# Attention over normalised queries and keys on one core: one reciprocal for both heads of a pair, and a new order

## The chip, the cores and the metric

The kernel runs on one core of a Trainium2 chip. The metric is the device time of the whole kernel in microseconds. The core has five engines that run side by side, each taking its own instructions strictly in order: TensorE (PE in the profile, its weight loads as PEld), VectorE (DVE), ScalarE (ACT), GpSimd (POOL) and SyncE (SP, which here only starts transfers). They wait for each other through semaphores.

## The reference

Eight batches of twelve heads, 512 positions, 64 dimensions, `tau` = 0.1:

```python
Q_norm = Q / (np.linalg.norm(Q, axis=-1, keepdims=True) + 1e-10)
K_norm = K / (np.linalg.norm(K, axis=-1, keepdims=True) + 1e-10)
scores = np.einsum('bhqd,bhkd->bhqk', Q_norm, K_norm) / tau
weights = np.exp(scores - np.max(scores, axis=-1, keepdims=True))
weights = weights / (np.sum(weights, axis=-1, keepdims=True) + 1e-10)
return np.einsum('bhqk,bhkd->bhqd', weights, V).astype(np.float32)
```

The scores are bounded by 10, so the kernel leaves out the maximum. It divides by the sum of the weights at the very end, after the product with V.

## The kernel before

**Tiling.** The 96 heads are worked off as 48 pairs of neighbouring heads, numbered 0 to 47 (`s` in the code; `h` is the head within a pair). 512 positions are four tiles of 128.

**One pair.** The steps have the names that the code gives them in `P.add`:

- `LD s.0`, `LD s.1`, `LV s` (SP): the transfers of Q, K and V into rings of buffers; a ring's size says how many pairs later a buffer is used again (`RINGS`: 17 for Q and K, 8 for V).
- `SQ` (POOL mostly), `SSQ` (PE, eight small products that sum the squares of K in groups) and `RED` (DVE): sums of squares. For Q, `RED` alone works on 512 columns.
- `NEW` steps (DVE, lines 419 to 430): the inverse root by Newton's method, for groups of two or four pairs at once, up to eight small instructions.
- `SCL s.0`, `SCL s.1` (DVE or POOL, line 451): scaling of Q and K. `TR s.0`, `TR s.1` (PE, line 457): four transposes each. `EVA s` (DVE, line 465): their copy out of PSUM.
- `SCO s.c` (PE, line 551), c = 0 to 3: scores of one key tile for both heads, two matmuls. `EXP s.c` (ACT, line 567): the exponential of those 128x1024 scores. Scores have four PSUM banks, so two chunks are held at a time. One chunk, `43.3`, is not done on ACT but as a polynomial on DVE and POOL (`SCX`, `X`, `Y`).
- `VC s` (POOL, line 575): V to bf16 with a column of ones next to the 64 of V.
- `PV s.h.i` (PE, line 587), i = 0 to 3: weights times V for one query tile, four matmuls of 65 columns. Column 65 is the sum of the weights. All four tiles of head h lie in one PSUM bank, `o_ps[h]`; the two banks are the halves of the tile `ops` (`both` in the code). The `SSQ` products use free columns of the same banks.
- `RCP s.h` (DVE, line 599): the reciprocal of the four sums of a head. `NRM s.h` (DVE, line 604): the product of the 128x256 result with them, into the buffer `ob` (a ring of 8). `ST s` (SP, line 608): the transfer of both heads to memory.

**What a bank waits for.** The first product of pair s + 1 in the bank of head h, `PV s+1.h.0`, waits for `NRM s.h` (and for a `RED`, where a sum of squares used that bank between). `NRM s.h` waits for `RCP s.h` and for the store of pair s - 8.

**The order.** Each engine's order is written out by hand in `ORDER` as numbers. A number is the place at which the step was registered by `P.add`, pair by pair. So the same number means another step once a registration is added or dropped. The prediction names the steps by what the numbers mean in each version, as `PV 36.0.2` for pair 36, head 0, query tile 2. `JOINT` and `ONE_PRODUCT` are lists of pairs that choose a form of `RCP` and `NRM`; before, `JOINT` is empty, and each head has its own `RCP`.

Of the kernel before, what the change touches and what calls it, by code (L numbers as in the profile page):

```python
# [5 lines left out]
ALU = mybir.AluOpType  # L6
# [102 lines left out]
def bass_cosine_similarity_attention_kernel(  # L109
# [8 lines left out]
    BATCH, NHEAD, SEQ, DIM = Q.shape  # L118
    assert SEQ == 512 and DIM == 64 and NHEAD % 2 == 0
    NT = SEQ // 128  # L120
# [4 lines left out]
    R_QK, R_V, R_VB, R_SQ, R_QN, R_QT, R_ET, R_O, R_X = RINGS  # L125
# [34 lines left out]
    P = Program(nc)  # L160
# [29 lines left out]

    def key(name, s, *rest):
        return (name, s) + rest if s >= 0 else None
# [48 lines left out]
    for s in range(NP):  # L241
        for h in range(2):
            bank_free[s, h] = before[h]
            before[h] = [("NRM", s, h)] + ([("RED",) + attached[s, h]] if (s, h) in attached else [])
# [282 lines left out]
    def rest(s):  # L527
# [54 lines left out]
        for h in range(2):  # L582
# [13 lines left out]
            ends = lambda h: [("PV", s, h, NT - 1), ("SSQ",) + attached[s, h] if (s, h) in attached else None, key("NRM", s - R_O, h)]  # L596
            if s not in JOINT:
                P.add(("RCP", s, h), "dve", "rcp", T0 + PERIOD + 0.9 * PV_AT[4 * h + 3] + late(s), ends(h),
                      lambda e, h=h, grid=grid: e.reciprocal(out=rd[io][:, h, :], in_=grid[:, :, DIM]))  # L599
            elif h == 0:  # L600
                P.add(("RCP", s), "dve", "rcp2", T0 + PERIOD + 0.9 * PV_AT[4 * h + 3] + late(s), ends(0) + ends(1),
                      lambda e: e.reciprocal(out=rd[io][:, :, :], in_=both[:, :, 0 : 65 * NT].rearrange("p h (t x) -> p h t x", x=65)[:, :, :, DIM]))
            P.add(("NRM", s, h), "dve", "nrm", T0 + PERIOD + 0.2 + 0.9 * PV_AT[4 * h + 3] + late(s), [("RCP", s) if s in JOINT else ("RCP", s, h), key("ST", s - R_O)],
# [3 lines left out]
        P.add(("ST", s), "sp", "ld", s + STORE_AT, [("NRM", s, i) for i in range(2)],  # L607
              lambda e: e.dma_start(out=src(out, s), in_=ob[io][:, :].rearrange("p h t d -> p h (t d)")), slot=f"out{io}")

    def last(s, T0):  # L610
        ivb, iet, io = s % R_VB, s % R_ET, s % R_O
        spare = t_ps[:, :, :, :].rearrange("p w t x -> p (w t x)").bitcast(f32)
        for k, (h, lo, hi) in enumerate(PIECES):
# [15 lines left out]
            P.add(("RCP", s, k), "dve", "rcp", T0 + PERIOD + 4 + k, [("PV", s, k, NT - 1), key("NRM", s - R_O, h)],  # L629
# [47 lines left out]
JOINT = ()  # L677
# [13 lines left out]
def late(s):  # L691
    return LATE * max(0.0, 1 - s / LATE_TO)


def slack(s, most):
# [14 lines left out]
    ),  # L710
    "pool": (
# [115 lines left out]
```

## Time and profile before

| | |
|---|---|
| median of 3 runs | 190.48 us (190.14 to 191.09) |
| the profiled execution | 190.63 us, of which the span (first to last instruction) 188.9 us |
| granted TensorE clock | 0.996 of full speed |
| memory | 37.75 MB read, 12.58 MB written, 267 GB/s over the span |
| transfers on SP's order | 193 |

A row of a group names the line, the engine, the operation, the tile written and the tiles read with their shapes, how often it ran, its busy time and mean duration in ns, and the idle time of the engine just before it, with what ended that. A row of the timeline has the start in us from the begin of the span, the length, and in brackets the idle time before. Instructions of one engine can overlap in their records, so the mean of a group can be longer than its share of the time.

### The profile page before, as it was taken

How to read it: one execution, taken by the hardware profiler on the slowest of the kernel's cores; microseconds unless marked ns; L12 is line 12 of the kernel's file. 1: busy time of each engine (PE TensorE's matmuls, PEld its weight loads, DVE VectorE, ACT ScalarE, POOL GpSimd, SP SyncE). 2: the span in 40 equal slices, each digit the busy share in tenths (PEclk: the TensorE clock that was granted, in tenths of full speed). 3: DMA queues.
4: the chain of work that ended last, by engine and by line, in shares of the span. 5: the costliest groups of instructions: out<-in, count | busy, mean ns of one | idle time of the engine just before them, and what ended most of it. 6: DMA issues, size and time to landing. Idle time of an engine off the chain costs nothing.

```text
span 188.9 us, 6666 instructions
## 1 busy us (share of the span) xinstructions
PE 175.7 (93%) x2710; PEld 111.0 (59%) x2710; DVE 169.3 (90%) x541; ACT 182.0 (96%) x214; POOL 160.9 (85%) x149
## 2 busy tenths in 40 slices
PE   8979889999999999999899989999999899899982
PEld 2545466656665666666566656656566566455652
DVE  1789999999999999999899998999989999998752
ACT  5699999999999999999999999999999999999993
POOL 3798999999999999999999999999999994594000
PEclk9999999999999999999999999999999999999998
DMA  5999999999997899999999999986973062200655
GB/s 182 346 353 351 349 350 374 367 378 271 293 313 264 263 310 318 263 351 357 377 363 326 374 358 365 362 302 193 333 267 115 2 222 88 86 0 3 207 186 168
DMA packets 52446, 50.76 MB, mean 269 GB/s; under 512 B 3136, under 2 KB 52416, under 8 KB 52416
## 3 DMA queue, kind: packets, MB, share of 16 engines
q1 hardware_dynamic: 51984, 50.02, 80.5%
q8 instruction: 21, 0.34, 0.8%
q10 hardware_dynamic: 432, 0.33, 0.5%
q14 instruction: 9, 0.07, 0.1%
HBM read 37.75 MB, written 12.58 MB: 267 GB/s over the span
## 4 chain that ended last, share of the span: by engine, by line
ACT 92%; PE 5%; DVE 2%; issue 0%
ACT et L567 89%; ACT et L543 2%; PE ops L205 2%; PE ops L587 1%; PE ops L619 0%; PE scps L551 0%; DVE ob L638 0%; PE tps L287 0%; PE ops L287 0%; ACT sq L360 0%; DVE xa L392 0%; DVE ob L604 0%; PE ops L385 0%; DVE qt L298 0%; DVE xa L269 0%
## 5 line engine op out<-in xcount | busy, mean ns | idle before, releaser
L567 ACT ACTIVATE et<-scps 128x1024 bf16<-128x1024 f32 x186 | 171.1, 1180 | 0.0
L368 POOL TENSOR_TENSOR sq<-qk 128x1024 bf16<-128x1024 f32 x44 | 82.7, 1893 | 0.4 <-DMA qk<-in_K_dram 0.3
L551 PE MATMUL scps<-qt 64*128 64x512 bf16 x374 | 73.0, 386 | 7.1 <-ACT et L567 3.6
L587 PE MATMUL ops<-vb,et 128*128 128x65 bf16 x1504 | 75.2, 195 | 0.5 <-DVE ob L604 0.3
L587 PEld LDWEIGHTS ops<-vb,et 128*128 128x128 bf16 x1504 | 57.1, 98 | 29.4 <-issue 17.7
L451 POOL TENSOR_TENSOR qn<-qk,rk 128x512 bf16<-128x512 f32 x38 | 39.2, 1043 | 6.4 <-DVE rk L426 6.2
L604 DVE TENSOR_TENSOR ob<-ops,rd 128x256 f32<-128x256 f32 x94 | 39.0, 419 | 1.2 <-DMA out_dram<-ob 0.5
L451 DVE TENSOR_TENSOR qn<-qk,nps 128x512 bf16<-128x512 f32 x56 | 36.9, 677 | 0.7 <-ACT nps L412 0.6
L465 DVE COPY qt<-tps 128x1024 bf16<-128x1024 bf16 x47 | 32.1, 683 | 0.8 <-PE tps L457 0.6
L457 PE MATMUL tps<-ident,qn 128*128 128x128 bf16 x376 | 32.3, 220 | 0.4 <-DVE qn L451 0.3
L551 PEld LDWEIGHTS scps<-qt 64*128 64x128 bf16 x374 | 18.4, 92 | 24.1 <-ACT et L567 8.0
L396 DVE TENSOR_REDUCE xs<-sq 128x8 f32<-128x512 bf16 x46 | 30.5, 671 | 0.2 <-POOL sq L368 0.2
L575 POOL TENSOR_SCALAR vb<-vf 128x512 bf16<-128x512 f32 x48 | 28.9, 620 | 0.2 <-DMA vf<-in_V_dram 0.2
L457 PEld LDWEIGHTS tps<-ident,qn 128*128 128x128 bf16 x376 | 21.5, 97 | 10.5 <-issue 5.2
L599 DVE RECIPROCAL rd<-ops 128x4 f32<-128x4 f32 x94 | 16.1, 174 | 5.0 <-PE ops L587 3.8
L385 PE MATMUL ops<-sq,ident 128*128 128x64 bf16 x384 | 19.0, 193 | 0.2 <-ACT sq L360 0.2
L385 PEld LDWEIGHTS ops<-sq,ident 128*128 128x128 bf16 x384 | 14.2, 98 | 4.1 <-issue 3.1
L392 DVE TENSOR_REDUCE xs<-ops 128x8 f32<-128x64 f32 x46 | 9.5, 207 | 0.6 <-PE ops L385 0.3
L419 DVE TENSOR_TENSOR ts<-xs,nps 128x32 f32<-128x32 f32 (+2 forms) x34 | 6.6, 194 | 0.6
L426 DVE SCALAR_TENSOR_TENSOR nps<-ts,nps 128x32 f32<-128x32 f32 (+3 forms) x34 | 6.7, 196 | 0.6
L422 DVE SCALAR_TENSOR_TENSOR ts<-ts,nps 128x32 f32<-128x32 f32 (+2 forms) x34 | 6.5, 190 | 0.4
L362 POOL TENSOR_TENSOR sq<-qk 128x512 bf16<-128x512 f32 x5 | 5.1, 1039 | 1.3 <-DMA qk<-in_K_dram 1.3
(62 smaller groups left out, 54.7 us busy)
## 6 DMA issues: line engine op xcount, KB each, us to landing
vf<-in_V_dram SPq DMA_DIRECT2D x48, 256.0 KB, 5.7
qk<-in_Q_dram SPq DMA_DIRECT2D x47, 256.0 KB, 4.8
qk<-in_K_dram SPq DMA_DIRECT2D x47, 256.0 KB, 5.6
out_dram<-ob SPq DMA_DIRECT2D x47, 256.0 KB, 4.7
qk<-in_Q_dram SPq DMA_DIRECT2D x2, 128.0 KB, 2.7
qk<-in_K_dram ACTq DMA_DIRECT2D x2, 128.0 KB, 2.9
out_dram<-ob SPq DMA_DIRECT2D x1, 128.0 KB, 1.7
out_dram<-ob ACTq DMA_DIRECT2D x1, 64.0 KB, 1.8
```

The source lines that it names most:

```text
L368: lambda e: e.tensor_tensor(out=sqf, in0=data, in1=data, op=ALU.mult))
L385: last = e.matmul(out=o_ps[bank][:, 320:384], lhsT=ident[:, :], rhs=sq[iqs][:, 8 * w : 8 * w + 8, 8 * k : 8 * k + 8], start=(k == 0), stop ...
L396: lambda e, w=w, dst=dst: e.tensor_reduce(out=dst, in_=sq[iqs][:, 8 * w : 8 * w + 8, :], axis=AX.X, op=ALU.add))
L451: lambda e, w=w, r=r: e.tensor_tensor(out=qn[iqn][:, w].rearrange("p t h d -> p h t d"), in0=qk[iq][:, w].rearrange("p h (t d) -> p h t d" ...
L457: last = e.transpose(t_ps[:, w, t, :], qn[iqn][:, w, t].rearrange("p h d -> p (h d)"), ident[:, :])
L465: lambda e: e.tensor_copy(out=qt[iqt][:, :, :, :].rearrange("p w t x -> p (w t x)"), in_=t_ps[:, :, :, :].rearrange("p w t x -> p (w t x)")))
L551: last = e.matmul(out=sc_ps[:, 2 * b + h, :], lhsT=qt[iqt][64 * h : 64 * h + 64, 1, c, :], rhs=qt[iqt][64 * h : 64 * h + 64, 0, :, :], sta ...
L567: lambda e, c=c, b=b: e.activation(out=et[iet][:, c, :, :], in_=sc_ps[:, 2 * b : 2 * b + 2, :], func=ACT.Exp, scale=math.log(2.0) / UNIT i ...
L575: lambda e: e.tensor_scalar(out=vb[:, ivb : ivb + n, :, :, 0:DIM].rearrange("p n h c d -> p (n h c) d"), in0=vf[:, iv : iv + n].rearrange( ...
L587: last = e.matmul(out=o_ps[h][:, 65 * t : 65 * t + 65], lhsT=et[iet][:, c, h, 128 * t : 128 * t + 128], rhs=vb[:, ivb, h, c, :], start=(c ...
L599: lambda e, h=h, grid=grid: e.reciprocal(out=rd[io][:, h, :], in_=grid[:, :, DIM]))
L604: lambda e, h=h, grid=grid: e.tensor_tensor(out=ob[io][:, h], in0=grid[:, :, 0:DIM], in1=rd[io][:, h, :].unsqueeze(2).to_broadcast([128, N ...
```

## The change

For pairs 12 to 45 there is one `RCP s` in place of `RCP s.0` and `RCP s.1`. It reads the sums of both heads, 128x8 values out of both banks, and waits for the last product of both. The two `NRM s.h` stay as they are, and both wait for the one `RCP s`. The form was in the code before (`if s not in JOINT`), with no pair in the list. The list `ONE_PRODUCT`, for one `NRM` over both heads as well, is new and empty, so that form isn't used. The helper `nrm` gives the name of the step that ends a pair's normalisation; with `ONE_PRODUCT` empty it gives what stood there before.

The orders of SP, POOL, DVE and PE are new from about the eighth pair on; ACT does the same steps in the same order as before. No transfer, product or POOL step is added or dropped. Some numbers of the lists change only because 34 registrations are gone.

```diff
+    def nrm(s, h):
+        return None if s < 0 else ("NRM", s, 0 if s in ONE_PRODUCT else h)
...
-            before[h] = [("NRM", s, h)] + ([("RED",) + attached[s, h]] if (s, h) in attached else [])
+            before[h] = [nrm(s, h)] + ([("RED",) + attached[s, h]] if (s, h) in attached else [])
...
-            ends = lambda h: [("PV", s, h, NT - 1), ("SSQ",) + attached[s, h] if (s, h) in attached else None, key("NRM", s - R_O, h)]
+            ends = lambda h: [("PV", s, h, NT - 1), ("SSQ",) + attached[s, h] if (s, h) in attached else None, nrm(s - R_O, h)]
             if s not in JOINT:
                 P.add(("RCP", s, h), "dve", "rcp", T0 + PERIOD + 0.9 * PV_AT[4 * h + 3] + late(s), ends(h),
                       lambda e, h=h, grid=grid: e.reciprocal(out=rd[io][:, h, :], in_=grid[:, :, DIM]))
             elif h == 0:
                 P.add(("RCP", s), "dve", "rcp2", T0 + PERIOD + 0.9 * PV_AT[4 * h + 3] + late(s), ends(0) + ends(1),
                       lambda e: e.reciprocal(out=rd[io][:, :, :], in_=both[:, :, 0 : 65 * NT].rearrange("p h (t x) -> p h t x", x=65)[:, :, :, DIM]))
...
-JOINT = ()
+JOINT = tuple(range(12, 46))
+ONE_PRODUCT = ()
```

Of the orders, the stretches that the prediction uses, in names:

| engine | before | after |
|---|---|---|
| PE, pair 36 to 37 | PV 36.0.2, PV 36.0.3, PV 35.1.2, PV 35.1.3, SCO 38.0, TR 39.0, TR 39.1, SCO 38.1, PV 37.0.0 | PV 36.1.2, PV 36.0.2, PV 36.0.3, PV 36.1.3, SCO 38.0, TR 39.0, TR 39.1, SCO 38.1, PV 37.0.0 |
| DVE, pair 36 | RCP 36.0, RCP 35.1, NEW, NRM 36.0, ..., RCP 36.1, SCL 40.0, NRM 36.1 | RCP 36, NEW, NEW, NRM 36.1, NRM 36.0 |
| SP, early | LV 5, LD 8.0, LD 8.1, LV 6, LD 9.0, LD 9.1, LV 7, LD 10.0, LD 10.1, LV 8 | LV 5, LD 11.1, LD 13.0, LD 8.0, LD 12.0, LD 8.1, LV 6, LD 9.0, LD 16.0, LD 9.1, LV 7, LD 10.0, LD 14.1, LD 17.1, LD 10.1, LD 21.1, LD 21.0, LD 15.0, LD 11.0, LD 16.1, LV 8 |
| SP, stores 9 to 14 in turn | 10, 9, 11, 13, 12, 14 | 12, 14, 9, 11, 10, 13 |
| POOL, pair 8 | SQ 10, VC 8, VC 6, VC 10, SCL 8.1 | SQ 10, VC 8, SCL 8.1 (VC 6 behind SQ 8, VC 10 later) |
| PE, end | SCO 47.1, PV 46.1.0, PV 46.0.0 to 46.0.3, SCO 47.2, PV 46.1.1 to 46.1.3, SCO 47.3, PV 47.1.0, PV 47.0.0, ... | SCO 47.1, PV 46.0.0, SCO 47.2, PV 46.0.1, PV 46.1.0, PV 46.0.2, PV 46.0.3, PV 46.1.1, SCO 47.3, PV 46.1.2, PV 46.1.3, PV 47.0.0, ... |

More of the change, by code (lines that the diff above doesn't have):

```diff
@@ L602, in rest @@
                       lambda e: e.reciprocal(out=rd[io][:, :, :], in_=both[:, :, 0 : 65 * NT].rearrange("p h (t x) -> p h t x", x=65)[:, :, :, DIM]))
+            if s in ONE_PRODUCT:
+                if h == 0:
+                    P.add(("NRM", s, 0), "dve", "nrm2", T0 + PERIOD + 0.2 + 0.9 * PV_AT[7] + late(s), [("RCP", s), key("ST", s - R_O)],
+                          lambda e: e.tensor_tensor(
+                              out=ob[io][:, :, :, :], in0=both[:, :, 0 : 65 * NT].rearrange("p h (t x) -> p h t x", x=65)[:, :, :, 0:DIM],
+                              in1=rd[io][:, :, :].unsqueeze(3).to_broadcast([128, 2, NT, DIM]), op=ALU.mult))
+                continue
             P.add(("NRM", s, h), "dve", "nrm", T0 + PERIOD + 0.2 + 0.9 * PV_AT[4 * h + 3] + late(s), [("RCP", s) if s in JOINT else ("RCP", s, h), key("ST", s - R_O)],
@@ L606, in rest @@
                       in1=rd[io][:, h, :].unsqueeze(2).to_broadcast([128, NT, DIM]), op=ALU.mult))
-        P.add(("ST", s), "sp", "ld", s + STORE_AT, [("NRM", s, i) for i in range(2)],
+        P.add(("ST", s), "sp", "ld", s + STORE_AT, [nrm(s, i) for i in range(2)],
               lambda e: e.dma_start(out=src(out, s), in_=ob[io][:, :].rearrange("p h t d -> p h (t d)")), slot=f"out{io}")
@@ L628, in last @@
             grid = bank[:, 0 : 65 * (hi - lo)].rearrange("p (t x) -> p t x", x=65)
-            P.add(("RCP", s, k), "dve", "rcp", T0 + PERIOD + 4 + k, [("PV", s, k, NT - 1), key("NRM", s - R_O, h)],
+            P.add(("RCP", s, k), "dve", "rcp", T0 + PERIOD + 4 + k, [("PV", s, k, NT - 1), nrm(s - R_O, h)],
                   lambda e, h=h, lo=lo, hi=hi, grid=grid: e.reciprocal(out=rd[io][:, h, lo:hi], in_=grid[:, :, DIM]))
```

149 rows, old and new, of the table ORDER are left out of this document.

## The prediction

> **What bounds the kernel now.** I read the page of the profile first: busy time by engine, then the chain that ended last, then the groups of instructions.
>
> ```profile
> span 188.9 us, 6666 instructions
> ...
> PE 175.7 (93%) x2710; PEld 111.0 (59%) x2710; DVE 169.3 (90%) x541; ACT 182.0 (96%) x214; POOL 160.9 (85%) x149
> ...
> DVE  1789999999999999999899998999989999998752
> ...
> ACT 92%; PE 5%; DVE 2%; issue 0%
> ...
> L567 ACT ACTIVATE et<-scps 128x1024 bf16<-128x1024 f32 x186 | 171.1, 1180 | 0.0
> ```
>
> Four engines look nearly full, but the chain runs through ACT for 92% of the span. Its exponentials (L567) fill 171.1 us with 0.0 us of idle time, so 171.1 / 186 = 0.920 us each. Their records (1180 ns) overlap, so a late one does not show as idle time: it shows as a longer step from start to start. For the best step I read two windows of ACT's timeline (start, length, group; each begins with the record already running):
>
> ```profile
> 99.94 11.18 ACT L567 ACTIVATE et<-scps 128x1024 bf16<-128x1024 f32 x12
> ```
> ```profile
> 108.97 2.15 ACT L567 ACTIVATE et<-scps 128x1024 bf16<-128x1024 f32 x2
> ```
>
> The first group has twelve starts and ends at 111.12, as the second does, so 108.97 is its eleventh: ten steps in 9.03 us, 0.903 each. All 186 at that step would take 168.0 us. **All that any rearrangement can win inside the exponentials is therefore 171.1 - 168.0 = 3.1 us.** The orders change from about 27 us on. The best case needs the share that lies there:
>
> ```profile
> 13.49 79.06 ACT et L567 x86
> ...
> 92.56 1.02 ACT et L567
> ...
> 93.60 88.11 ACT et L567 x96
> ```
>
> These are pieces of the chain in order of time. The first 15 of the 186 start before 27 us. The later 171 carry about their part of the 3.1 us or a little less; adding up their single steps gives 2.4 us over 0.903. I use 2.4 us as the ceiling of a gain there. The run took 190.63 us around its span of 188.9; the median of the three runs shown is 190.48, 0.15 below it. Sums below are made on 190.63 and given against the median.
>
> **Where the 2.4 us go.** The worst single one is at 91 us. ACT's, DVE's and TensorE's timelines there:
>
> ```profile
> 91.33 2.25 ACT L567 ACTIVATE et<-scps 128x1024 bf16<-128x1024 f32 x2
> ```
> ```profile
> 91.02 0.42 DVE L604 TENSOR_TENSOR ob<-ops,rd 128x256 f32<-128x256 f32 x1 [0.48 <-DMA out_dram<-ob]
> ```
> ```profile
> 91.51 0.68 PE L587 MATMUL ops<-vb,et 128*128 128x65 bf16 x16 [0.34 <-DVE ob L604]
> 92.12 0.39 PE L551 MATMUL scps<-qt 64*128 64x512 bf16 x2
> ```
>
> The normalisation of pair 20 waits 0.48 us for the store of pair 12 to leave its buffer (the ring `ob` has 8). TensorE's products wait for it, the scores behind them run at 92.12, and the exponentials step from 91.33 to 92.56 and on to 93.60 (above), 1.23 and 1.04 us: 0.46 us lost. The other 1.9 us are many small losses where TensorE's work between two score products is longer than 0.903:
>
> ```profile
> 177.29 0.39 PE L551 MATMUL scps<-qt 64*128 64x512 bf16 x2
> 177.62 0.68 PE L587 MATMUL ops<-vb,et 128*128 128x65 bf16 x16
> 178.23 0.39 PE L551 MATMUL scps<-qt 64*128 64x512 bf16 x2
> 178.56 0.62 PE L457 MATMUL tps<-ident,qn 128*128 128x128 bf16 x8
> 179.11 0.39 PE L551 MATMUL scps<-qt 64*128 64x512 bf16 x2
> ```
>
> From start to start: a score chunk takes 0.32 to 0.33 us of TensorE, 16 products (four PV operations) 0.61, eight transposes 0.55. A score chunk with 16 products is 0.94, over ACT's 0.903. TensorE is the second bound.
>
> **Part 1: one reciprocal for two.**
>
> ```profile
> L599 DVE RECIPROCAL rd<-ops 128x4 f32<-128x4 f32 x94 | 16.1, 174 | 5.0 <-PE ops L587 3.8 <-PE ops L385 0.5
> L604 DVE TENSOR_TENSOR ob<-ops,rd 128x256 f32<-128x256 f32 x94 | 39.0, 419 | 1.2 <-DMA out_dram<-ob 0.5
> L392 DVE TENSOR_REDUCE xs<-ops 128x8 f32<-128x64 f32 x46 | 9.5, 207 | 0.6 <-PE ops L385 0.3
> L419 DVE TENSOR_TENSOR ts<-xs,nps 128x32 f32<-128x32 f32 (+2 forms) x34 | 6.6, 194 | 0.6
> ```
>
> Thirty-four pairs lose two reciprocals of 174 ns and get one of 128x8 over both banks, which no row shows. Its bounds are 174 ns (eight columns as cheap as four) and 348 (as dear as two). The nearest rows are small DVE operations on the same engine, 194 ns for 32 columns and 207 for a reduction to eight; I take 195. DVE is relieved of 34 x (348 - 195) = 5.2 us, between 0 and 5.9. None of it lies on the chain: ACT hides it, and DVE holds 2% of the chain. So its direct value is **0**; indirectly it can only cut into the 2.4 us.
>
> [...]
>
> **Part 2: what the reciprocal now waits for.** Before, each head's bank went alone through its own last product, reciprocal (0.21 to the next start), normalisation (0.42), and back to TensorE, while TensorE worked into the other bank. Now both wait for the later head's last product, and one bank waits for two normalisations. The price is set by TensorE's work between the last product of pair s and the first of pair s + 1 in a bank (the room) against DVE's chain there (the need).
>
> ```profile
> 178.34 0.18 DVE L599 RECIPROCAL rd<-ops 128x4 f32<-128x4 f32 x1 [0.30 <-PE ops L587]
> 178.55 0.42 DVE L604 TENSOR_TENSOR ob<-ops,rd 128x256 f32<-128x256 f32 x1
> ```
>
> The next TensorE work could start at 178.23 (above) and the reciprocal starts at 178.34: 0.11 for the signal. The way back was 91.44 to 91.51: 0.07. Together 0.18.
>
> Pair 36 worked out. Before, PE has PV 36.0.2, 36.0.3, 35.1.2, 35.1.3, then SCO 38.0, TR 39.0, TR 39.1, SCO 38.1, PV 37.0.0: room 0.31 + 0.32 + 0.55 + 0.32 = 1.50. DVE has RCP 36.0, RCP 35.1, one NEW step, NRM 36.0: 0.21 + 0.21 + 0.21 + 0.42 + 0.18 = 1.23. It fits. After, PV 36.1.3 closes the pair, then SCO 38.0, TR 39.0, TR 39.1, SCO 38.1, PV 37.0.0: room 1.19. DVE has RCP 36, two NEW steps, NRM 36.1, NRM 36.0: 0.21 + 0.42 + 0.84 + 0.18 = 1.65. TensorE comes up **0.46 us short**.
>
> ```profile
> 83.10 0.40 PE L385 MATMUL ops<-sq,ident 128*128 128x64 bf16 x8
> 83.33 0.29 PE L587 MATMUL ops<-vb,et 128*128 128x65 bf16 x4
> ```
> ```profile
> L465 DVE COPY qt<-tps 128x1024 bf16<-128x1024 bf16 x47 | 32.1, 683 | 0.8 <-PE tps L457 0.6
> ```
>
> I did the same for both heads of pairs 12 to 45, with 0.15 us for one PV operation, 0.25 for a sum of squares (0.23 from start to start here), 0.68 for the large DVE operations, and no two scores closer than 0.903. The mean room falls from 1.99 to 1.58 us; the mean DVE chain goes from 1.06 to 1.10. Before, 6 of 68 hand-overs are short, by 1.3 us in all; after, 15 are, by 3.6 us. Extra: 2.3 us of TensorE waits. Of such a wait, the slack of the slots takes a part: a slot's mean TensorE work is 0.86 us against 0.903 in both orders, so a pair brings back about 0.16 us. Bounds for ACT: 0 (all absorbed) and +2.3. The trace of before shows only one such wait reaching TensorE, that at 91 us, although six were short by this count; so I lean to the lower end and take **+0.7**.
>
> **Part 3: the new orders.** The number of transfers, products and POOL operations is the same; ACT's order of work is the same. SP's order moves the store of pair 12 ahead of those of 9, 10, 11 and 13 and of the V loads of 21 to 28, which frees its buffer earlier: the 0.46 us at 91 us can go. Late stores of others can come instead (SP issues the store of 9 behind that of 14), but the buffer is needed three pairs later, 12 exponentials or 11 us. I take **-0.5**, bounds -2.4 and +1.4 (three such waits). One early risk: eleven loads of pairs 11 to 21 now stand ahead of the V load of pair 8, which moves from the 9th to the 20th place behind the V load of pair 5.
>
> ```profile
> 20.94 0.66 SPq L345 DMA_DIRECT2D vf<-in_V_dram  x1
> ...
> 29.43 0.47 SPq L342 DMA_DIRECT2D qk<-in_Q_dram  x1
> ```
> ```profile
> 34.47 1.78 POOL L575 TENSOR_SCALAR vb<-vf 128x512 bf16<-128x512 f32 x3
> ```
> ```profile
> vf<-in_V_dram SPq DMA_DIRECT2D x48, 256.0 KB, 5.7
> ```
>
> The 9th place was issued at 20.94, the 20th at 29.43. With 5.7 us it lands at about 35.1, and POOL's cast of pair 8 ran at 34.47; POOL would stand 0.6 us, but the casts of 6 and 10 (0.6 each) no longer stand between it and the scaling of key 8. I take 0, at most +0.6.
>
> ```profile
> 184.17 1.32 ACT L562 ACTIVATE et<-scps 128x512 bf16<-128x512 f32 x3
> ```
> ```profile
> 184.44 0.35 PE L619 MATMUL ops<-vb,et 128*128 128x65 bf16 x6 [0.41 <-DVE ob L604]
> ```
>
> The tail: TensorE now does head 0 of pair 47 before head 1, which takes away its 0.41 us wait for the last normalisation of pair 46. But the last exponentials end at 184.17 + 1.32 = 185.49 and the last product can't come sooner, and five PV operations instead of three stand before the last score chunk (0.3 us more). Net 0, plus or minus 0.2.
>
> **Sum:** 0 + 0.7 - 0.5 + 0 = +0.2 us. On 190.63 that is 190.8; against the median, 190.7. **I forecast no change that can be measured, 190.7 us.** About 0.5% (0.95 us) is what a measurement of this kernel can tell from no change.
>
> **Rivals.**
> *Slower by the hand-over.* Place: first product of a pair in each bank (L587), behind the last normalisation. It decides if the extra shortage exceeds some 1.2 us unabsorbed; in full it gives 190.5 + 2.3 = 192.8. For it: the room shrinks by 0.4 us on average, and TensorE slots of 0.94 leave nothing to catch up. Against: one visible wait in before. Chance 0.24. [...]
> *Slower by transfers.* Three waits like that of 91 us, 0.46 each: 191.9. Chance 0.10.
> *Faster by a freed DVE.* With 5.2 us less work, DVE is early everywhere, and 1 to 2.4 us of the small losses go: 188.1 to 189.5, say 189.1. For it: DVE is at nine tenths or more in most of the 40 slices (first fence). Against: most lost slots are TensorE's own 0.94 to 1.0, which DVE doesn't shorten. Chance 0.20.
> *The joint reciprocal costs as much as two.* DVE saves nothing: 190.7 to 191.4. It counts within my forecast's chance.
>
> **How the numbers follow.** Forecast 0.46 (189.5 to 191.4 alone); slower 0.34; faster 0.20. For eight in ten I leave out the far ends of both sides: 189.2 to 192.4.
>
> **What would show it.** L599 in two forms with some 195 ns for 128x8; ACT's L567 still at 0.0 idle with 171 to 172 us in all; TensorE waits for L604 in more places than one, after pairs 12, 14, 24, 36, 42 and 45; no wait of L604 for a store at pair 20. L567 near 169 us would prove me wrong on the one side, above 173 on the other.

## The result, and the profile after

The changed kernel takes 192.0 us (median of 5 runs, 191.74 to 192.44) against 190.48: 1.0081 times as long, with a 95% interval of 1.0062 to 1.0099. It is slower by 1.5 us; the forecast was no change that can be measured.

The page of the profile after (the profiled execution took 192.30 us; lines of the code stand 3 to 10 lower than before, so L567 is now L570, L604 is L614, L575 is L578, L587 is L590):

```profile
span 190.5 us, 6641 instructions
...
PE 176.8 (93%) x2710; PEld 110.8 (58%) x2710; DVE 168.2 (88%) x507; ACT 183.1 (96%) x214; POOL 161.2 (85%) x149
...
PE 37%; ACT 32%; DVE 23%; POOL 4%; issue 2%; POOLq 0%
...
L570 ACT ACTIVATE et<-scps 128x1024 bf16<-128x1024 f32 x186 | 172.1, 1091 | 0.3
...
L578 POOL TENSOR_SCALAR vb<-vf 128x512 bf16<-128x512 f32 x48 | 29.3, 621 | 3.0 <-DMA vf<-in_V_dram 1.2
...
L605 DVE RECIPROCAL rd<-ops 128x8 f32<-128x8 f32 x34 | 6.9, 204 | 6.4 <-PE ops L590 5.2
```

ACT still shows almost no idle time, yet the chain no longer runs along ACT for 92% of the span but for 32%; the rest goes over TensorE, DVE and POOL. So ACT is now released late in many places, though the chain doesn't say by how much. POOL stood idle for 3.0 us before its casts of V (L578); in the kernel before, that group had 0.2:

```profile
L575 POOL TENSOR_SCALAR vb<-vf 128x512 bf16<-128x512 f32 x48 | 28.9, 620 | 0.2 <-DMA vf<-in_V_dram 0.2
```

Where the time went is read from the starts of the exponentials. All steps from one start to the next, less 0.903 us each (0.9035 with one more digit), added up by stretch (worked out from the starts in the traces, one profiled execution of each kernel):

| lost between exponentials, us | 0 to 27 | 27 to 39 | 39 to 60 | 60 to 100 | 100 to 120 | 120 to 145 | 145 on | sum |
|---|---|---|---|---|---|---|---|---|
| before | 0.39 | 0.24 | 0.10 | 0.94 | 0.25 | 0.33 | 0.52 | 2.8 |
| after | 0.39 | 0.65 | 0.10 | 1.10 | 0.52 | 0.93 | 0.50 | 4.2 |

That is 1.4 us; the step to the last, divided exponential grew from 0.92 to 1.07. Together 1.6, the whole difference of the spans (190.5 - 188.9). Head and end are alike: the last divided exponential starts 4.69 us before the end in the one and 4.74 in the other.

Two stretches stand out. The first, in POOL's timeline:

```profile
28.78 0.62 POOL L578 TENSOR_SCALAR vb<-vf 128x512 bf16<-128x512 f32 x1 [0.55 <-PE ops L388]
29.36 2.04 POOL L454 TENSOR_TENSOR qn<-qk,rk 128x512 bf16<-128x512 f32 x2
31.36 3.74 POOL L371 TENSOR_TENSOR sq<-qk 128x1024 bf16<-128x1024 f32 x2
36.32 0.62 POOL L578 TENSOR_SCALAR vb<-vf 128x512 bf16<-128x512 f32 x1 [1.21 <-DMA vf<-in_V_dram]
36.90 1.04 POOL L454 TENSOR_TENSOR qn<-qk,rk 128x512 bf16<-128x512 f32 x1
```

These are the casts of V of pairs 7 and 8. The load of pair 8 was issued at 29.37 us and landed at 36.24; that of pair 7 landed at 28.70, so the 0.55 us are a wait for it too, although the row names another releaser. The steps behind these two casts lose 0.25 us (at 30.1) and 0.17 (at 37.7). Behind each cast in POOL's order stands a scaling of a key (L454), and the chain shows what hangs on it:

```profile
28.78 0.62 POOL vb L578
29.40 1.01 POOL qn L454
30.41 0.05 issue
30.46 0.40 PE tps L460 x4
30.86 0.34 PE scps L554 x2
31.20 0.02 issue
31.22 1.02 ACT et L570
```

Cast, scaling, transposes, scores, exponential. The second stretch begins in SP's order:

```profile
100.98 0.48 SPq L618 DMA_DIRECT2D out_dram<-ob  x1
101.50 8.97 SPq L345 DMA_DIRECT2D qk<-in_Q_dram  x2
110.51 0.47 SPq L618 DMA_DIRECT2D out_dram<-ob  x1
```
```profile
100.00:110.00 10.00, 9.50 (x155) 6.07 (x156) 8.81 (x26) 10.00 (x12) 9.93 (x9) 1.00 0.55 183
```

Two Q loads, those of pairs 38 and 45, with 8 us between them. The load of pair 45 waits for the buffer of pair 28, which is free when its query is scaled at 110.1. Its first consumer, the squares of pair 45 on POOL, starts at 136.86, but everything behind it in SP's order waits too; the transfers fall to 183 GB/s in this stretch (last column, of the view by windows), and what piled up goes out at once: eight transfers are issued from 110.51 to 114.21. The V load of pair 35, issued at 113.71, lands at 121.69, 8.0 us later, and POOL stands until then, although the row again names another releaser:

```profile
118.67 1.89 POOL L371 TENSOR_TENSOR sq<-qk 128x1024 bf16<-128x1024 f32 x1
121.77 0.62 POOL L578 TENSOR_SCALAR vb<-vf 128x512 bf16<-128x512 f32 x1 [1.21 <-DVE ts L425]
122.35 1.89 POOL L371 TENSOR_TENSOR sq<-qk 128x1024 bf16<-128x1024 f32 x1
124.20 1.04 POOL L454 TENSOR_TENSOR qn<-qk,rk 128x512 bf16<-128x512 f32 x1
```

From 121.77 to 147 us POOL has no pause of 0.1 us in which to catch up. The step at 125.4 us loses 0.25, and those at 139.5 and 140.6 lose 0.34 together; the chain to the exponential at 140.58 runs through POOL's key scaling at 138.76. POOL had little to spare in the kernel before either: its 85% is an average over a span at whose end it is idle, and in the 40 slices of before it is busy for nine tenths or more from 19 to 156 us.

```profile
POOL 3798999999999999999999999999999994594000
```

### The profile page after: what moved, and what is told of

Its sections match the earlier page's. It is cut to its first block, busy times and chain, and to the rows that moved or that the text cites. A ratio compares the mean times of both kernels' runs of the same rounds, so it can differ in the third digit from the quotient of the medians.

```text
span 190.5 us, 6641 instructions
## 1 busy us (share of the span) xinstructions
PE 176.8 (93%) x2710; PEld 110.8 (58%) x2710; DVE 168.2 (88%) x507; ACT 183.1 (96%) x214; POOL 161.2 (85%) x149
## 4 chain that ended last, share of the span: by engine, by line
PE 37%; ACT 32%; DVE 23%; POOL 4%; issue 2%; POOLq 0%
ACT et L570 31%; PE ops L590 14%; PE scps L554 11%; DVE ob L614 5%; PE tps L460 5%; DVE qn L454 4%; DVE qt L468 3%; PE ops L388 3%; DVE xs L399 3%; PE ops L208 2%; POOL sq L371 2%; DVE ts L422 1%; DVE xs L395 1%; DVE ts L425 1%; DVE nps L429 1%
## 5 line engine op out<-in xcount | busy, mean ns | idle before, releaser
L570 ACT ACTIVATE et<-scps 128x1024 bf16<-128x1024 f32 x186 | 172.1, 1091 | 0.3
L590 PE MATMUL ops<-vb,et 128*128 128x65 bf16 x1504 | 75.4, 195 | 2.0 <-DVE ob L614 0.8
L590 PEld LDWEIGHTS ops<-vb,et 128*128 128x128 bf16 x1504 | 57.0, 98 | 31.3 <-issue 20.0
L454 POOL TENSOR_TENSOR qn<-qk,rk 128x512 bf16<-128x512 f32 x38 | 39.3, 1044 | 4.0 <-DVE rk L429 3.9
L614 DVE TENSOR_TENSOR ob<-ops,rd 128x256 f32<-128x256 f32 x94 | 37.4, 419 | 0.7
L454 DVE TENSOR_TENSOR qn<-qk,nps 128x512 bf16<-128x512 f32 x56 | 37.2, 678 | 0.8 <-ACT nps L415 0.6
L460 PE MATMUL tps<-ident,qn 128*128 128x128 bf16 x376 | 32.9, 220 | 1.7 <-POOL qn L454 0.9
L578 POOL TENSOR_SCALAR vb<-vf 128x512 bf16<-128x512 f32 x48 | 29.3, 621 | 3.0 <-DMA vf<-in_V_dram 1.2
L605 DVE RECIPROCAL rd<-ops 128x8 f32<-128x8 f32 x34 | 6.9, 204 | 6.4 <-PE ops L590 5.2
```

The lines of the kernel that those rows point to most:

```text
L454: lambda e, w=w, r=r: e.tensor_tensor(out=qn[iqn][:, w].rearrange("p t h d -> p h t d"), in0=qk[iq][:, w].rearrange("p h (t d) -> p h t d" ...
L460: last = e.transpose(t_ps[:, w, t, :], qn[iqn][:, w, t].rearrange("p h d -> p (h d)"), ident[:, :])
L570: lambda e, c=c, b=b: e.activation(out=et[iet][:, c, :, :], in_=sc_ps[:, 2 * b : 2 * b + 2, :], func=ACT.Exp, scale=math.log(2.0) / UNIT i ...
L578: lambda e: e.tensor_scalar(out=vb[:, ivb : ivb + n, :, :, 0:DIM].rearrange("p n h c d -> p (n h c) d"), in0=vf[:, iv : iv + n].rearrange( ...
L590: last = e.matmul(out=o_ps[h][:, 65 * t : 65 * t + 65], lhsT=et[iet][:, c, h, 128 * t : 128 * t + 128], rhs=vb[:, ivb, h, c, :], start=(c ...
L614: lambda e, h=h, grid=grid: e.tensor_tensor(out=ob[io][:, h], in0=grid[:, :, 0:DIM], in1=rd[io][:, h, :].unsqueeze(2).to_broadcast([128, N ...
```

## The experiments

Theory T: the loss comes from V loads that stand too late in SP's new order; POOL's casts wait for them, and the key scalings behind the casts come late. Theory H, the rival of the prediction: it comes from the hand-over of the two banks behind the joint reciprocal. All ratios are to the kernel before, on the same chip.

**The old order of transfers in the changed kernel, and the reverse.** `a1_sp` has SP's order from before and everything else as changed; `a4_sppool` the opposite, with POOL's order too.

> The changed kernel with SP's order of transfers as it was before; reciprocals, DVE, PE, POOL and ACT orders as changed. Theory T (the loss comes from V loads that stand later in SP's order, so that POOL's casts wait and the key scalings behind them are late): the waits of POOL for V at pairs 7, 8 and 35 (0.55, 1.21 and 1.20 us) go, L570 falls from 172.1 to about 171, and the time to 190.8 to 191.2. Theory H (the loss comes from the hand-over of the two banks behind the joint reciprocal): 192.0, unchanged within 0.3.

> The kernel before (own reciprocals, its PE, DVE and ACT orders) with the SP and POOL orders of the change. Theory T: most of the loss comes along, 191.3 to 192.0, with POOL waiting for V loads at pairs 7 and 8. Theory H: 190.5 within 0.4.

Measured: 209.61 us (1.0967, 1.0926 to 1.1008) and 212.99 (1.1189, 1.1151 to 1.1227). Both theories missed by 17 us and more. The orders are tuned to each other, and a foreign one stops whole engines; for `a1_sp`, the waits of DVE and of ACT:

```profile
DVE ob L614 <- DMA out_dram<-ob: 8.7, 3, 6.1
```
```profile
ACT et L570 <- PE scps L554: 15.6, 8, 7.9
```

A normalisation (pair 33, head 0) waits up to 6.1 us for a store (pair 25, issued at 146.13 us) that the old order issues later than the new DVE order needs it. These two say nothing on T or H; only small edits can.

**Separate reciprocals in the changed orders.** DVE's order around pair 36, as an example of all 34:

```diff
-RCP 36, NEW, NEW, NRM 36.1, NRM 36.0
+RCP 36.1, NEW, NEW, NRM 36.1, RCP 36.0, NRM 36.0             a2_split
+RCP 36.1, RCP 36.0, NEW, NEW, NRM 36.1, NRM 36.0             c4_bothwait
```

> All orders as changed, but each head has its own reciprocal again, placed right before its own normalisation, so that the first head no longer waits for the second's last product and DVE has its 5 us back. Theory H: TensorE's waits for L614 shrink and the time falls by 0.5 us or more, to 191.5 or less. Theory T: within 0.3 of 192.0, if anything slower by the DVE work.

> The orders of the change, loads not moved, with two reciprocals side by side at the joint one's place, that of the head that ends later first. So both heads wait as with the joint reciprocal, and DVE has its 5 us back. The run with each reciprocal at its own normalisation measured 194.67. Theory H (waiting for both heads is dear): this one is slower than that by 0.5 or more, 195.2 or above. Theory D (waiting for both costs nothing in these orders, and what they lack is DVE time): 194.7 within 0.4.

Measured: `a2_split` 194.67 us (1.0217, 1.0188 to 1.0246), `c4_bothwait` 192.77 (1.0136, 1.0093 to 1.0180). All four forecasts missed: both theories had `a2_split` at 192.3 or less, and `c4_bothwait` at 194.3 or more. The one in which both heads wait is the faster of the two, so H in its plain form falls: waiting for both heads isn't what makes the difference between them. DVE's timeline at pair 36 shows why; changed kernel, then `c4_bothwait`, then `a2_split`:

```profile
150.30 0.21 DVE L605 RECIPROCAL rd<-ops 128x8 f32<-128x8 f32 x1 [0.35 <-PE ops L590]
150.42 0.17 DVE L425 SCALAR_TENSOR_TENSOR ts<-ts,nps 128x64 f32<-128x64 f32 x1
150.63 0.19 DVE L429 SCALAR_TENSOR_TENSOR rk<-ts,nps 128x32 f32<-128x32 f32 x1
150.73 0.75 DVE L614 TENSOR_TENSOR ob<-ops,rd 128x256 f32<-128x256 f32 x2
```
```profile
150.85 0.25 DVE L602 RECIPROCAL rd<-ops 128x4 f32<-128x4 f32 x2 [0.35 <-PE ops L590]
151.02 0.19 DVE L425 SCALAR_TENSOR_TENSOR ts<-ts,nps 128x64 f32<-128x64 f32 x1
151.24 0.19 DVE L429 SCALAR_TENSOR_TENSOR rk<-ts,nps 128x32 f32<-128x32 f32 x1
151.35 0.75 DVE L614 TENSOR_TENSOR ob<-ops,rd 128x256 f32<-128x256 f32 x2
```
```profile
152.13 0.18 DVE L602 RECIPROCAL rd<-ops 128x4 f32<-128x4 f32 x1 [0.35 <-PE ops L590]
152.23 0.19 DVE L425 SCALAR_TENSOR_TENSOR ts<-ts,nps 128x64 f32<-128x64 f32 x1
152.45 0.19 DVE L429 SCALAR_TENSOR_TENSOR rk<-ts,nps 128x32 f32<-128x32 f32 x1
152.56 0.42 DVE L614 TENSOR_TENSOR ob<-ops,rd 128x256 f32<-128x256 f32 x1
152.89 0.17 DVE L602 RECIPROCAL rd<-ops 128x4 f32<-128x4 f32 x1
```

From the first reciprocal to the end of the second normalisation: 151.48 - 150.30 = 1.18 us with the joint one, 152.10 - 150.85 = 1.25 with two side by side. With the second one between the normalisations, its start alone is 0.76 after the first reciprocal, and 0.2 to the normalisation and 0.42 of its own follow: about 1.4. So at this pair a joint reciprocal saves 0.07 us against two neighbours, not the 0.14 that the durations promise: the records of independent neighbours overlap, 0.25 us for the two reciprocals in `c4_bothwait`. And a reciprocal right ahead of the normalisation that needs it lengthens the hand-over here, to those 1.4 us. In `a2_split` TensorE waits for L614 in 7 places, 2.3 us in all. Both runs keep the late V loads of pairs 7 and 8 in their traces (POOL stands 0.6 and 1.4 us in each), so their times hold that loss too. The changed kernel differs from `c4_bothwait` in the one reciprocal alone; it is faster by the medians (1.0081 against 1.0136), but the intervals overlap.

**The joint reciprocal in the old orders.** Of the 34 pairs, 12 have the first head of the next pair started, in the PE order of before, ahead of this pair's last product; there a joint reciprocal needs a new PE order (and in pair 15 a new DVE order). The other 21 can have it.

```diff
-RCP 24.0, RED, NRM 24.0, NEW, NEW, RCP 24.1, NEW, NRM 24.1
+RED, NEW, NEW, RCP 24, NRM 24.0, NEW, NRM 24.1
```

> The kernel before with the joint reciprocal in 21 pairs (17 to 19, 21 to 26, 28 to 30, 32 to 34, 40 to 45), those in which its PE order lets both heads end before the next pair begins; the reciprocal stands at the place of the later of the two, and the earlier head's normalisation moves right behind it. All other orders as before. Theory H: slower by at least half of the 1.5 us, 191.2 or more, with TensorE waiting for L614. Theory T: 190.5 within 0.4.

Measured: 194.33 us (1.0194, 1.0166 to 1.0223), 3.6 us slower. TensorE's and ACT's waits from 27 to 186 us:

```profile
PE ops L590 <- DVE ob L614: 4.4, 8, 1.1
```
```profile
ACT et L570 <- PE scps L554: 2.8, 6, 1.0
```

Here H holds: the hand-over reaches TensorE (4.4 us; before, 0.3 in one place) and ACT. SP's, POOL's and PE's orders are those of the kernel before here, and POOL waits for no V load. The mechanism is real, and an order made without it pays 3.6 us. The new orders exist to make room for it, and the question is what they left of it.

**Three transfers moved in the changed kernel.** SP's order:

```diff
-... LD 38.0, LD 45.0, ST 20, LD 42.1, LV 32, LD 39.1, LD 43.0, LV 33, LV 35, LD 45.1 ...
+... LD 38.0, ST 20, LD 42.1, LV 32, LD 39.1, LD 43.0, LV 33, LV 35, LD 45.0, LD 45.1 ...    b1_ld45
-... LV 6, LD 9.0, LD 16.0, LD 9.1, LV 7, LD 10.0, ..., LD 16.1, LV 8 ...
+... LV 6, LV 7, LD 9.0, LD 16.0, LD 9.1, LV 8, LD 10.0, ..., LD 16.1 ...                    b2_v78
```

> The changed kernel with one transfer moved: the Q load of pair 45, at which SP waits from 102 to 110 us for its buffer, goes eleven places later, right ahead of the K load of pair 45. Theory T (late V loads hold POOL, and the key scalings behind it hold TensorE): the loads behind it start up to 8 us earlier, POOL's wait of 1.20 us before the cast of pair 35 goes, and with it the late exponentials at 125 us (0.25) and 139 to 141 us (0.34): 0.4 to 0.6 us faster than the changed kernel's 192.0, so 191.4 to 191.6. Theory H (the loss is the hand-over of the banks behind the joint reciprocal, and POOL's wait is covered): 192.0 within 0.3.

> The changed kernel with two transfers moved: the V load of pair 7 right behind that of pair 6, and the V load of pair 8 right behind the K load of pair 9, ten places earlier. Theory T: POOL's waits of 0.55 us before the cast of pair 7 and 1.21 us before that of pair 8 go, the exponentials between 30 and 39 us lose 0.24 us in all as in the kernel before and not 0.65: 191.6. Theory H: 192.0 within 0.3.

> Both of these together in the changed kernel, three transfers moved and nothing else. Theory T: about 1.0 us faster than the changed kernel, 190.9 to 191.2, so that little of the 1.5 us is left. Theory H: 191.7 or more.

Measured: `b1_ld45` 191.62 us (1.0065, 1.0040 to 1.0091), `b2_v78` 191.90 (1.0069, 1.0047 to 1.0091), `b3_both` 191.22 (1.0045, 1.0027 to 1.0063). (Counted in the lists, the Q load of pair 45 moves by seven places and the V load of pair 8 by nine, not by the eleven and ten of the expectations.) The first meets T's 191.4 to 191.6 within its spread. The second misses T's figure by 0.3 by its median, which lies where H had it (192.0 within 0.3); its six runs fall in two groups, 191.1 to 191.2 and 191.9 to 192.05. Neither interval is clear of that of the changed kernel (1.0062 to 1.0099). Both together come to 191.2, T's upper end and outside H's range. The profiles, one execution of each, say where:

| lost between exponentials, us | 27 to 39 | 60 to 100 | 100 to 120 | 120 to 145 | 145 on | all |
|---|---|---|---|---|---|---|
| before | 0.24 | 0.94 | 0.25 | 0.33 | 0.52 | 2.8 |
| after | 0.65 | 1.10 | 0.52 | 0.93 | 0.50 | 4.2 |
| load of 45 moved | 0.59 | 1.05 | 0.52 | 0.18 | 0.69 | 3.5 |
| V loads of 7 and 8 moved | 0.30 | 1.14 | 0.52 | 0.17 | 0.69 | 3.3 |
| both | 0.26 | 1.04 | 0.52 | 0.18 | 0.69 | 3.1 |

Each edit takes away the loss of its own stretch. For the load of pair 45 the transfers show how. In `b1_ld45` the V load of pair 35 is issued no earlier (113.48 us, against 113.71), but what stood ahead of it has gone by then:

```profile
100.00:110.00 10.00, 9.51 (x160) 6.25 (x158) 8.65 (x25) 10.00 (x12) 9.93 (x10) 1.00 0.96 327
```

These are 327 GB/s against 183 after the change, and the load lands 2.8 us after its issue, at 116.28, where it took 8.0. Moving the V loads of 7 and 8 emptied the stretch at 120 to 145 us as well, in the execution that was profiled (191.14 us, of the lower group). There the load of pair 45 still holds SP until 109.55, the V load of pair 35 lands at 120.32, and POOL stands 0.39 us for it and not 1.21, which ACT doesn't notice. So the wait there is a close race. That the slower executions lose it would fit the two groups of its times, but no trace shows one. With both, no wait for a V load is left in POOL's list. It now has, from 25 to 40 us,

```profile
POOL qn L454 <- DVE rk L429: 1.1, 1, 1.1
```

a wait for DVE that costs ACT nothing that can be seen (0.26 lost in that stretch, 0.24 before the change). T explains 1.0 of the 1.4 us lost between the exponentials, and 0.7 us of the time by the ratios (1.0081 to 1.0045; the intervals just touch). The profile flatters it: of `b3_both` one of the fastest executions was profiled (190.99 us; its twelve lie between 190.94 and 192.41), of the changed kernel one of the slower (192.30).

**What is left: 0.4 us between exponentials, 0.15 at the last step; 0.9 us by the medians (1.0045).** Two edits on top of `b3_both`:

```diff
-PE:  SCO 47.2, PV 46.0.1, PV 46.1.0, PV 46.0.2, PV 46.0.3, PV 46.1.1, SCO 47.3, ...
+PE:  SCO 47.2, PV 46.0.1, PV 46.1.0, PV 46.0.2, SCO 47.3, PV 46.0.3, PV 46.1.1, ...   c1_tail
-DVE: RCP 36, NEW, NEW, NRM 36.1, NRM 36.0
+DVE: RCP 36, NRM 36.1, NRM 36.0, NEW, NEW                                            c2_close
```

> The changed kernel with the three loads moved as in the run with both, and two PV operations of pair 46 (0.3 and 1.1) moved behind the last score chunk, which leaves three ahead of it as in the kernel before. If the long last step of the exponentials (1.07 us, chunk 47.2 to 47.3) comes from these, it falls to 0.92 to 0.95 and the time by 0.1 to 0.2: 191.0 to 191.1. If the products pushed behind become the end, 191.2 to 191.4.

> The changed kernel with the three loads moved, and in the 11 pairs (12, 14, 16, 20, 24, 28, 34, 35, 36, 39, 40) in which DVE's order has NEW steps or a scaling between the joint reciprocal and the second normalisation, these 23 instructions moved right behind it, so that the banks come free up to 0.8 us earlier. Theory H' (what is left over the kernel before is the hand-over): 0.3 to 0.5 us faster, 190.7 to 190.9. Theory T' (the hand-over is covered, what is left is length of TensorE's slots): 191.2 within 0.25, or slower where the moved steps were due.

> All of it: three loads, the two PV operations and the 23 DVE instructions. If each holds by itself, 190.5 to 190.8, the kernel before; if only the loads count, 191.2 within 0.25.

`c1_tail`: 191.61 us (1.0061, 1.0043 to 1.0079), above both of its forecasts, and not to be told from `b3_both`. Its last step is back at 0.92 us, but the end after it grew from 4.75 to 5.18, because the normalisation of pair 46 came later and a product of pair 47 (L629) waited for it:

```profile
PE ops L629 <- DVE ob L614: 0.4, 1, 0.4
```

The long last slot was the price of a shorter end. This trace also shows that the three moves don't end the late V loads: SP's order is that of `b3_both`, yet POOL stands 0.87 us for the V load of pair 24 (issued at 94.81, landed at 102.33), and the exponentials lose 0.48 us at 102.4. In the trace of `b3_both` the same wait is 0.12 us and costs nothing. `c2_close`: 193.96 (1.0183, 1.0160 to 1.0207), 2.7 us slower than `b3_both` (T' had allowed for slower, H' had not), and `c3_all` 194.33 (1.0203, 1.0173 to 1.0232) with it, off both of its forecasts. The steps of the inverse root between reciprocal and normalisation were not idle ballast: set behind, they come late for the scalings of queries and keys, and POOL waits for the result in more places (6, against 3 in `b3_both`, from 40 to 160 us):

```profile
POOL qn L454 <- DVE rk L429: 2.5, 6, 0.6
```

TensorE waits 0.61 and 0.70 us, at 144.9 and 170.0, for the two query scalings that were among the 23 (pairs 37 and 44), and 0.74 for a normalisation at 177.75. So what the hand-over still costs can't be had back in this way. The waits of TensorE of over 0.1 us before products, from 27 to 182 us, are 0.53 (at 72 us), 0.14, 0.20, 0.15 and 0.11 us after the change, 1.1 in all, against 0.34 and 0.14 before; `b3_both` has the same five. They are the likely rest of the loss, beside such V loads as that of pair 24 in slower executions. No run took them away alone (in `c2_close` the 0.53, 0.14 and 0.20 are still there), so that part is argued, not shown.

**The store of pair 12 in the kernel before.**

```diff
-ST 11, ST 13, LV 26, LD 30.0, LD 30.1, LV 27, LV 28, LD 31.0, LD 31.1, ST 12
+ST 11, ST 12, ST 13, LV 26, LD 30.0, LD 30.1, LV 27, LV 28, LD 31.0, LD 31.1
```

> The kernel before with one transfer moved: the store of pair 12 goes right behind that of pair 11, ten places earlier. If the 0.46 us lost at 91 us hang on that store alone, L567 falls by 0.3 to 0.46 us and the time to 190.0 to 190.2; if another wait takes its place, 190.5 within 0.2.

Measured: 190.52 us, 0.9995 (0.9981 to 1.0009), the second branch of the expectation. (The store moves by eight places, not ten.) The wait at 91 us is gone, and the loss from 60 to 100 us falls from 0.94 to 0.64, but the exponentials gained only 0.23 us in all and the time nothing that can be told. No version beat the kernel before.

## Why the time fell inside the range and the figure was missed

The sum was +0.2 us and the measured change is +1.5. The 192.0 us lie inside 189.2 to 192.4 only because that range was kept wide for the slower rivals; they lie outside the 189.5 to 191.4 of the forecast itself. That the range held is luck as far as the mechanism goes.

- **The bound.** Right. ACT's exponentials at 0.903 us were the floor in both kernels (the best ten steps in a row take 9.03 us in the trace of either); all of the 1.6 us is ACT released late, in the steps and at the last one.
- **Part 1, the reciprocal.** Its duration was forecast at 195 ns and is 204. The relief was over-stated: 34 x (348 - 204) = 4.9 us by durations, but DVE's busy time fell by 1.1 (169.3 to 168.2), and at pair 36 the joint one saves 0.07 us against two neighbours, which would be 2.4 us for 34 such pairs. "Direct value 0" held. The 0.07 us are saved on an engine that isn't the bound.
- **Part 2, the hand-over, taken as +0.7.** Mechanism right: in the old orders it costs 3.6 us for 21 pairs. There TensorE stood 4.4 us for the normalisations behind the joint reciprocal (`a3_joint`), against 0.3 before. In the new orders its upper bound was too large. Pair 36 was to come up 0.46 us short, and TensorE stood 0.08 us there. The need was counted as 1.47 us from reciprocal to the second normalisation's end; it is 1.18, since the two normalisations together take 0.75, not 0.84, and independent neighbours start 0.10 to 0.12 apart, not 0.21. All in all TensorE's extra waits are 1.1 - 0.5 = 0.6 us, not 2.3. They come behind pairs 14, 22, 23, 24 and 44; of the pairs named, 14 and 24 are among them. At most 0.4 us of them show between the exponentials, or 0.6 if the 0.2 that the earlier store of pair 12 may have won is added back. So +0.7 was not far off.
- **Part 3, the new orders, taken as -0.5.** This is the step that failed. Its gain came (no normalisation waits for a store at pair 20 any more), but `b4_st12` shows that this gain is worth 0.2 us and not 0.46. Its loss was seen in part and priced at nothing. The V load of pair 8 was forecast to be issued at 29.43 and was issued at 29.37; it landed not at 35.1 but at 36.24, 6.9 us later. The row's 5.7 us is a median of the whole run; the V loads of pairs 4 to 9, issued from 11 to 23 us, took 7.1 to 8.5 us in the same trace of before, which the prediction did not read. And "the casts of 6 and 10 no longer stand between" was taken as enough cover, but the scaling of key 8 began at 36.90 us, where it had begun at 36.35. The V load of pair 7, behind which the exponentials lost more (0.25 us against 0.17), was not looked at. Nor was the load of pair 45 that holds up SP for 8 us, although it is in the order. Together these three places are the 1.0 us that moving three loads won back. The rival *slower by transfers* named the class and had a chance of 0.10; but its 191.9 us were three waits of DVE for stores, and what came were waits of POOL for loads, so that its figure is close is luck too.
- **The tail.** "Plus or minus 0.2": it was +0.15 in the last step, +0.05 behind it. Its 0.41 us wait behind pair 46 went, and one of 0.44 behind pair 45 came in its place.

## What to carry to other kernels

A new order has to be read queue by queue, also for the engine that only issues transfers: look for a transfer that waits for its buffer long before it is due, since everything behind it waits too (8 us here, behind the load of pair 45), and ask when the first consumer stands still. Take the time to landing from transfers of the same stretch, not from the median of the run (here 6.9 and 8.0 us against 6.3), and ask whether the consumer has any time in hand there. Price a small instruction by the distance to the next start, not by its duration (the joint reciprocal: 0.12 us to an independent successor, at a duration of 0.21). If an engine's steps are interleaved, moving one out of a critical pair can cost more than the pair gains (`c2_close`: 2.7 us slower than `b3_both`).

## What was not expected

- A V load of 256 KB took 6.9 us (pair 8, 348 GB/s from 27 to 37 us) and 8.0 us (pair 35, 312 GB/s from 113 to 122) from issue to landing, against a median of 5.7 before and 6.3 after. The same load of pair 35 took 2.8 us in `b1_ld45`, where 152 GB/s moved from 110 to 120, against 260 after the change.
- Two normalisations of 0.42 us side by side take 0.75; an independent successor of a reciprocal of 0.18 to 0.21 us starts 0.10 to 0.12 us after it. The four columns of the second bank add 30 ns to the duration of a reciprocal (174 to 204).
- Orders that were found together could not be mixed here: SP's alone, taken from the other kernel, cost 17.6 us (`a1_sp`, 209.61 us against 192.0).
